# Two-choice mixture of experts on one core: result rows written straight to their tokens' places, and read in plain transfers at the end

## The chip, the cores and the metric

The kernel runs on one core of a Trainium2 chip. Its engines are TensorE (PE), VectorE (DVE), ScalarE (ACT), GpSimd (POOL) and SyncE (SP); 16 DMA engines serve it. SP and POOL issue the transfers. The metric is the device time of one execution in microseconds (us). A measurement of this kernel is the median of its runs.

## What is computed

A token block of 512 x 1024 floats runs through two blocks. The first is a conformer-like block (convolution, latent attention, convolutional feed-forward). The second has attention over selected keys, a gated delta rule, and a mixture of experts in two levels. The change lies in that last part. Cut to it, the reference is:

```python
top_gp, g_idx = lax.top_k(p_grp, 1)                       # one of 4 groups
top_pe, e_local = lax.top_k(softmax(in_grp), 2)           # 2 of its 8 experts
gates = top_pe / sum(top_pe) * top_gp
e_idx = g_idx * 8 + e_local                               # [512, 2]
...
hb = silu(xb @ w_gate[e]) * (xb @ w_up[e])                # each expert, on its tokens
yb = (hb @ w_down[e]) * gate
out = zeros(...).at[token].add(yb)                        # both choices of a token
...
x = layer_norm(alpha * x + (1 + gt2) * out, ln_g, ln_b)
```

Each of the 32 experts has three matrices of 2 MB (gate and up 1024 x 512, down 512 x 1024), 201 MB together, and each is used once.

## The kernel before

**Places.** Routing (`routing`, to L1740) gives every expert CAP = 64 places. Choice j of token p in token block t (4 blocks of 128) gets the row number `rows_i[p, j, t]`, cast at L1730: expert times 64 plus its rank among that expert's tokens. An expert with more than 64 tokens goes on in a loop behind (`overflow`, L1819, a `For_i` at L1823 with a run-time count, which starts with a barrier of all engines); there are 15 spare blocks for it.

**Expert loop** (from L1846). One pass per expert. `gate_up` (L1774) multiplies the tokens of the expert with the gate and up weights, 32 matmuls at L1782 (`gu`), and applies the activation (ACT L1787, DVE L1788). `down` (L1792) of the expert before is woven in: transposes (L1796), matmuls at L1805 (`py`), then the product with a modulation row into half of a 128 x 1024 tile `ey` (DVE L1811), which holds both experts of a pair. Weights come through `ld` and `ew` (L1556 to L1580): 12 tiles of 512 KB per expert, 384 in all, issued by SP (L1563 gate and up, L1565 down) into `eraw` buffers in the order of their use, each when its buffer is free and at most eight in flight. `ahead(e, n)` issues the first n of them early; before the overflow loop, at expert 16, it issues 15 tiles.

**Results.** `y_d` in DRAM has one row for each of the (32 + 15) x 64 places. At step i == 7 of every even expert from 2 on, POOL writes the `ey` tile of the pair before with one plain transfer of 512 KB (L1896), empty places too: 15 writes. The last pair (experts 30 and 31) stays on chip: it is split into two parts (`yh`, `yl`) and brought to its tokens by one-hot matmuls. Rows from 15 x 128 on, which this pair and the spare blocks would have, were filled with zeros much earlier by two transfers on SP (L918).

**Tail** (from L1915). Behind the last write, POOL issues eight gathers (L1920): for token block t and choice j, 128 rows of `y_d` picked by `rows_i` into a tile `ya`. `add(t, j)` (DVE L1925) adds gate times `ya` to the residual `x`. For t = 0 and 1 the second choice goes over PE instead, as a multiplication with a diagonal matrix of the gates (`dg`, L1941, into the accumulator `fin`). `sums(t)` adds the last pair's rows (L1946) and `x` (L1948) there. Then moments (DVE L1955), the norm (L1964 on), and `finish(t)` (ACT L1977, DVE L1978 and L1979, output by SP at L1980).

What sets the order: each engine works its own list in program order; SP's list holds the weight tiles and at its end the outputs, POOL's the writes and gathers.

Of the kernel before, what the change touches and what calls it, by code (L numbers as in the profile page):

```python
# [20 lines left out]
S = 512  # L21
# [28 lines left out]
def tile_model(ctx: ExitStack, tc: tile.TileContext, A: dict, out: bass.AP):  # L50
# [38 lines left out]
    def r(ap):  # L89
        return ap.bitcast(F32R)  # L90
# [820 lines left out]
            yield c  # L911


    y_d = dram.tile([(32 + 15) * 64, D], F32, name="y_d")
    zt = ch("zt")
    GP.memset(zt, 0.0)
    for hf in range(2):
        SY.dma_start(y_d[15 * P :, hf * S : (hf + 1) * S].rearrange("(a p) n -> p a n", p=64),  # L918
                     zt[:64, :].rearrange("p (o n) -> p o n", o=1).to_broadcast([64, 17, S]))

# [379 lines left out]
                    topk_some(1)  # L1302
    topk_some(1000)

    ckv = []
    for j in range(2):
        ps = col_T(w2, 1024 + j * P, h, "ckv")
# [383 lines left out]
    def routing():  # L1691

        ge, gs, e2 = rt(4, "ge"), rt(1, "gs"), rt(1, "e2")
        tc.keep_in_program_order(V.tensor_tensor(ge, gl, bc(gm, 4), ALU.subtract))
        SC.activation(ge, ge, AF.Exp)
        tc.keep_in_program_order(V.tensor_tensor(e2, m2, m1, ALU.subtract))
        SC.activation(e2, e2, AF.Exp)
        tc.keep_in_program_order(V.tensor_reduce(gs, ge, axis=AX.X, op=ALU.add))
        V.reciprocal(gs, gs)
        tc.keep_in_program_order(V.tensor_scalar(gate1, e2, 1.0, None, ALU.add))  # L1700
        V.reciprocal(gate1, gate1)
        V.tensor_tensor(gate1, gate1, gs, ALU.mult)
        V.tensor_tensor(gate2, gate1, e2, ALU.mult)

        nbi = rs_(NE).bitcast(I32)
        nb = rs_(NE)
        V.tensor_scalar(nb, pc, -1.0, 0.0, ALU.add, ALU.max)
        V.tensor_copy(nbi, nb)
        V.tensor_scalar(nbi, nbi, 6, None, ALU.arith_shift_right)
        V.tensor_copy(nb, nbi)  # L1710
        oend = [nb, rs_(NE), rs_(NE)]
        cur = 0
        for i, sft in enumerate((1, 2, 4, 8, 16)):
            nxt = 1 + i % 2
            V.tensor_copy(oend[nxt][:, :sft], oend[cur][:, :sft])
            V.tensor_tensor(oend[nxt][:, sft:], oend[cur][:, sft:], oend[cur][:, : NE - sft], ALU.add)
            cur = nxt
        oe = oend[cur]

        obase = rs_(NE)  # L1720
        V.tensor_tensor(obase, oe, nb, ALU.subtract)
        V.tensor_scalar(obase, obase, float(CAP), float(NE * CAP - CAP), ALU.mult, ALU.add)
        V.tensor_tensor(obase, obase, sbase, ALU.subtract)
        V.tensor_scalar(rowt, rk, float(CAP), None, ALU.is_ge)
        V.tensor_tensor(rowt, rowt, b3(obase), ALU.mult)
        V.tensor_tensor(rowt, rowt, rankf, ALU.add)
        for j in range(2):
            V.tensor_tensor(rj[j], rowt, E[j], ALU.mult)
            V.tensor_reduce(rowf[:, j, :], rj[j], axis=AX.X, op=ALU.add)
        V.tensor_copy(rows_i, rowf)  # L1730

        ovf = small(16, "ovf")[0:1, :]
        ovc = rs_(NOV * NE)[0:1].rearrange("p (b e) -> p b e", b=NOV)
        V.tensor_tensor(ovc, oe[0:1, :].rearrange("p (o e) -> p o e", o=1).to_broadcast([1, NOV, NE]),
                        iota[0:1, :NOV].rearrange("p (b o) -> p b o", o=1).to_broadcast([1, NOV, NE]), ALU.is_le)
        V.tensor_reduce(ovf[:, 0:NOV], ovc, axis=AX.X, op=ALU.add)
        V.tensor_scalar(ovf[:, 0:NOV], ovf[:, 0:NOV], float(NE - 1), None, ALU.min)
        V.tensor_copy(ovf[:, 15:16], oe[0:1, NE - 1 : NE])
        V.tensor_copy(ovi, ovf)
        V.tensor_scalar(relv, rflat, -float(NE * CAP), None, ALU.add)  # L1740

    gate1, gate2 = rt(1, "gate1", keep=True), rt(1, "gate2", keep=True)
    rowf = cpool.tile([P, 2, NT], F32, name="rowf")
# [76 lines left out]
    def overflow():  # L1820

        n_ov = nc.values_load(ovi[0:1, 15:16], min_val=0, max_val=NOV)
        with tc.For_i(0, n_ov, 1) as ib:  # L1823
            ei = nc.values_load(ovi[0:1, bass.ds(ib, 1)], engines=(mybir.EngineType.SP,), min_val=0, max_val=NE - 1)
            dyn = lambda w, q: ew({"g": wg, "u": wu, "d": wd}[w][bass.ds(ei, 1)].rearrange("o k n -> (o k) n"), 1 if w == "d" else 2, q, loop=True)
            xo, go = [], []
            run(gather(relv, 1, xo))
            run(gate_up(dyn, (xo[0], 0), go))
            yo = ytile()
            run(down(dyn, go[0], yo[:CAP, :]))  # L1830
            SY.dma_start(y_d[bass.ds(ib * CAP + NE * CAP, CAP), :], yo[:CAP, :])
            V.tensor_scalar(relv, relv, -float(CAP), None, ALU.add)

    def residual():
# [15 lines left out]
    for e in range(NE):  # L1850
# [31 lines left out]
            next(gx[0])  # L1882
            next(gx[0])
        if e == E_OV:
            ahead(e, 15)
            overflow()
            gx.append(gather(rel_cols((e // 4 + 1) * 4 * CAP), 4, xg))
        load = lambda w, q, e=e: ld(w, e, q)
        gu = gate_up(load, (xg[e // 4], e % 4), g)
        for i in range(8):  # L1890
            next(gu)
            if i == 2 and e:
                downs.append(down(loadp, gp, yp, rg=rgs[:, 0:1] if e == NE - 1 else None))
            downs = [d for d in downs if next(d, 1) is None]
            if i == 7 and e and e % 2 == 0:
                GP.dma_start(y_d[(e - 2) * CAP : e * CAP, :], yd)  # L1896
            if e >= E_RES and i % 4 == 3:
                next(res_, None)
            n = e % 4 * 8 + i
            if e == 0:  # L1900
                if i < 3:
                    next(gx[0])
                    next(gx[0])
            elif e < NE - 4 and (n >= 20 if e < 4 else n % 3 == 0):
                next(gx[-1], None)
# [11 lines left out]
    for t in range(NT):  # L1917
        for j in range(2):
            ya = pp("pa" if j == 0 else "pb", "ya")
            GP.indirect_dma_start(out=ya, out_offset=None, in_=y_d, in_offset=bass.IndirectOffsetOnAxis(ap=rows_i[:, j, t : t + 1], axis=0))  # L1920
            yas.append(ya)

    def add(t, j):
# [12 lines left out]
            split_to(yh[q, hs], yl[q, hs], y[q, hs])  # L1936
    pf = {(t, half): mm("fin") if t < 2 else acc("fin") for t in range(NT) for half in range(2)}
    HS = [slice(half * S, (half + 1) * S) for half in range(2)]
    for t in range(2):
        for half in range(2):  # L1940
            kp(PE.matmul(pf[t, half], lhsT=dg[:, cs[t]], rhs=yas[2 * t + 1][:, HS[half]], start=True, stop=False))  # L1941

    def sums(t):
        for half in range(2):
            for i, yy in enumerate((yh, yl)):
                kp(PE.matmul(pf[t, half], lhsT=r(ohT)[:, cs[t]], rhs=r(yy)[:, HS[half]], start=t > 1 and i == 0, stop=False))  # L1946
        for half in range(2):
            kp(PE.matmul(pf[t, half], lhsT=ident, rhs=x_sb[t][:, HS[half]], start=False, stop=True))  # L1948

# [29 lines left out]
            V.tensor_tensor(f, f, lb2[:, hs], ALU.add)  # L1979
            SY.dma_start(out[0, t * P : (t + 1) * P, hs], f)  # L1980

    for j in range(2):
        add(2, j)
    sums(0)
    moments(0)
    for j in range(2):
        add(3, j)
    sums(1)
    moments(1)
    norm((0, 1))  # L1990
    for t in (2, 3):
        sums(t)
        moments(t)
    finish(0)
    norm((2, 3))
    for t in (1, 2, 3):
# [15 lines left out]
```

## Time and profile before

| | us |
|---|---|
| runs | 2093.14, 2095.64, 2089.97 (median 2093.14) |
| profiled execution | 2092.43 |
| its span in the trace | 2090.7 |
| PE busy | 1988.3 (95%) |
| VectorE busy | 1241.0 (59%) |
| ScalarE busy | 756.4 (36%) |
| POOL busy | 78.4 (4%) |

The span is the time from the first to the last record of the profiled execution; the execution's own time is 1.7 us longer. "Busy" is an average over stages with different limits. The share of DMA in a window is the mean busy share of the 16 DMA engines; full engines show a share slightly over 1. "<-" behind an idle time names what ended it.

### The profile page before, as it was taken

Reading aid. Unit: us, or ns where it says so; the run is one execution under the profiler, and the core shown is the slowest. Engines: PE = TensorE matmul, PEld = TensorE weight load, DVE = VectorE, ACT = ScalarE, POOL = GpSimd, SP = SyncE. Lnnn points to the kernel's source line nnn. Section 1 sums busy time; section 2 is a strip of 40 time slices with the busy share of each in tenths; the row PEclk is TensorE's granted clock in tenths of the full one; section 3 lists DMA queues with packets and bytes.
Section 4 is the critical chain, followed back from the end, with each engine's and each line's share of the span. In section 5 each row is a group of like instructions: output and inputs, shape, how many; then the busy total and the mean of one; then the engine's idle time right before and its main releaser. Section 6 shows DMA issues by size and latency. Waiting matters only on the chain. (4 is left out here: it accounts for less than half of the span.)

```text
span 2090.7 us, 25944 instructions
## 1 busy us (share of the span) xinstructions
PE 1988.3 (95%) x9522; PEld 1397.1 (67%) x9522; DVE 1241.0 (59%) x2824; ACT 756.4 (36%) x1401; POOL 78.4 (4%) x110
## 2 busy tenths in 40 slices
PE   7999989999999999999999999999979999799985
PEld 6887658877877778888878877778754334333322
DVE  4898666688558747889999553443562221242216
ACT  5433873343223336755546234552230000000001
POOL 1000000000000011000000000010100000000001
PEclk9999999999999999999999999999989999899998
DMA  4443005366446335632232323133179999999994
GB/s 132 107 106 82 30 21 164 109 199 185 150 133 183 124 104 136 167 80 56 75 80 71 85 78 84 51 102 99 54 264 419 406 419 419 369 419 419 419 420 193
DMA packets 306342, 377.05 MB, mean 180 GB/s; under 512 B 45829, under 2 KB 225549, under 8 KB 306213
## 3 DMA queue, kind: packets, MB, share of 16 engines
q1 hardware_dynamic: 301748, 359.12, 50.6%
q0 software_dynamic: 4464, 16.25, 2.0%
q8 instruction: 76, 1.25, 0.2%
q14 instruction: 54, 0.43, 0.1%
HBM read 354.06 MB, written 21.26 MB: 180 GB/s over the span
## 5 line engine op out<-in xcount | busy, mean ns | idle before, releaser
L100 DVE TENSOR_TENSOR wl<-wraw,wh 128x1024 fp32r<-128x1024 f32 (+1 forms) x196 | 236.9, 1210 | 210.4 <-ACT wh L99 209.6
L99 ACT CAST wh<-wraw 128x1024 fp32r<-128x1024 f32 (+1 forms) x196 | 202.7, 1037 | 396.6 <-PE up L130 72.8
L1782 PE MATMUL gu<-eraw,xs 128*64 128x512 f32 x1024 | 316.1, 605 | 17.4 <-SPq L1823 11.8
L1782 PEld LDWEIGHTS gu<-eraw,xs 128*64 128x64 f32 x1024 | 83.0, 137 | 146.4 <-issue 109.2
L129 PE MATMUL pc<-hi,wh 128*128 128x512 f32 (+2 forms) x480 | 176.9, 374 | 0.8 <-ACT hi L99 0.4
L130 PE MATMUL pc<-lo,wh 128*128 128x512 f32 (+2 forms) x480 | 173.3, 364 | 0.5 <-DVE lo L100 0.5
L131 PE MATMUL pc<-hi,wl 128*128 128x512 f32 (+2 forms) x480 | 172.8, 362 | 0.0
L1805 PE MATMUL py<-eraw,ehT 128*64 128x512 f32 x512 | 162.5, 600 | 6.2 <-DMA eraw<-in_w_down_dram 4.6
L1788 DVE TENSOR_TENSOR eg<-gu,eg 64x512 f32<-64x512 f32 x32 | 22.2, 693 | 208.8 <-ACT eg L1787 208.5
L129 PE MATMUL up<-hi,wh 128*128 128x512 f32 x328 | 130.9, 399 | 0.0
L130 PE MATMUL up<-lo,wh 128*128 128x512 f32 x328 | 129.7, 395 | 0.0
L131 PE MATMUL up<-hi,wl 128*128 128x512 f32 x328 | 129.7, 395 | 0.0
L1787 ACT ACTIVATE eg<-gu 64x512 f32<-64x512 f32 x32 | 18.9, 589 | 279.0 <-PE gu L1782 279.0
L131 PEld LDWEIGHTS pc<-hi,wl 128*128 128x128 f32 (+1 forms) x480 | 90.1, 188 | 12.6
L129 PEld LDWEIGHTS pc<-hi,wh 128*128 128x128 f32 (+1 forms) x480 | 90.0, 189 | 12.6 <-ACT hi L99 1.0
L130 PEld LDWEIGHTS pc<-lo,wh 128*128 128x128 f32 (+1 forms) x480 | 90.4, 189 | 11.3 <-DVE lo L100 0.7
L1805 PEld LDWEIGHTS py<-eraw,ehT 128*64 128x64 f32 x512 | 45.1, 137 | 76.3 <-issue 56.7
L450 DVE SCALAR_TENSOR_TENSOR u<-u,cols_dw 128x497 f32<-128x497 f32 (+14 forms) x120 | 84.9, 753 | 0.7
L1770 ACT ACTIVATE xs<-xg,pb,pg 128x256 f32<-128x256 f32 x32 | 18.1, 564 | 177.8 <-PE xg L1766 161.7
L1766 PEld LDWEIGHTS xg<-oh,zNh 128*128 128x128 f32 x224 | 42.5, 190 | 53.1 <-issue 38.9
L129 PEld LDWEIGHTS up<-hi,wh 128*128 128x128 f32 x328 | 61.6, 188 | 23.8 <-ACT wh L99 7.8
L1772 DVE TENSOR_SCALAR xs<-xg,pg,pb 128x256 f32<-128x256 f32 x32 | 17.4, 543 | 95.4 <-PE xg L1766 95.3
(616 smaller groups left out, 4375.9 us busy)
## 6 DMA issues: line engine op xcount, KB each, us to landing
eraw<-in_w_gate_dram SPq DMA_DIRECT2D x128, 512.0 KB
eraw<-in_w_up_dram SPq DMA_DIRECT2D x128, 512.0 KB
eraw<-in_w_down_dram SPq DMA_DIRECT2D x128, 512.0 KB
wraw<-in_w_in_dram SPq DMA_DIRECT2D x91, 512.0 KB
wada<-in_w_ada_dram SPq DMA_DIRECT2D x48, 512.0 KB
wraw<-in_w_ffn_up_dram SPq DMA_DIRECT2D x44, 512.0 KB
wraw<-in_w_ffn_down_dram SPq DMA_DIRECT2D x20, 512.0 KB
wraw<-in_w_out_dram SPq DMA_DIRECT2D x16, 512.0 KB
```

The source lines that it names most:

```text
L99: c = SC.copy(r(hi), src)
L100: (eng or V).tensor_tensor(r(lo), src, hi, ALU.subtract)
L129: PE.matmul(ps, lhsT=wh, rhs=xh, start=start, stop=False)
L130: PE.matmul(ps, lhsT=wh, rhs=xl, start=False, stop=False)
L131: PE.matmul(ps, lhsT=wl, rhs=xh, start=False, stop=stop)
L450: yield lambda j=j, lo=lo, hi=hi, s=s: V.scalar_tensor_tensor(a[:, lo:hi], u[:, lo + s : hi + s], dww[:, j * 4 + c : j * 4 + c + 1], a[:, ...
L1766: PE.matmul(ps[:, :n], lhsT=hN[t][s_][:, c * P : (c + 1) * P], rhs=r(ov[:, t, :]), start=t == 0 and s_ == 0, stop=t == NT - 1 and s_ == 1)
L1770: SC.activation(xs[:, c], pv, AF.Identity, scale=pg[:, c : c + 1], bias=pb[:, c : c + 1])
L1782: PE.matmul(ps[m * CAP : (m + 1) * CAP, :], lhsT=xs[0][:, 2 * q + k, xs[1], :], rhs=rw[m][:, k * S : (k + 1) * S], start=q == 0 and k == 0 ...
L1787: SC.activation(g[CAP:, :], ps[:CAP, :], AF.Silu)
L1788: V.tensor_tensor(g[:CAP, :], ps[CAP:, :], g[CAP:, :], ALU.mult)
L1805: PE.matmul(py[half * CAP : (half + 1) * CAP, :], lhsT=hT[:, c * CAP : (c + 1) * CAP], rhs=raw[:, half * S : (half + 1) * S], start=c == 0 ...
```

## The change

`y_d` becomes 1024 rows, one for each choice of each token: row 2 x token + j. A table `tab_d` in DRAM with one integer per place says which row a place belongs to. It is filled with 2048, beyond the last row (1023), near the start of the second block. In `routing`, eight indirect writes put the row numbers of 128 tokens each into the table, and one read brings the first 2048 entries on chip as `tab` (128 x 16, a column per pair). The write of a pair (`put`, L1762 of the changed kernel) is an indirect write by such a column with a bounds check: a place whose entry is out of range is skipped. The zero fill covers all of `y_d`, moves behind the delta rule's stage and goes by POOL's queue. The tail reads `y_d` with eight plain transfers on SP, issued behind the last weight tile. On PE the second choice of all four token blocks goes over the diagonal matrix, and VectorE adds only the first choice. Before the overflow loop 13 tiles are issued ahead instead of 15. In that loop the write goes by the table too.

```diff
-    y_d = dram.tile([(32 + 15) * 64, D], F32, name="y_d")
+    y_d = dram.tile([2 * S, D], F32, name="y_d")
+
+    NROWS = (32 + 15) * 64
+    tab_d = dram.tile([NROWS, 1], I32, name="tab_d")
     zt = ch("zt")
     GP.memset(zt, 0.0)
-    for hf in range(2):
-        SY.dma_start(y_d[15 * P :, hf * S : (hf + 1) * S].rearrange("(a p) n -> p a n", p=64),
-                     zt[:64, :].rearrange("p (o n) -> p o n", o=1).to_broadcast([64, 17, S]))
+    ft = ch("ft").bitcast(I32)
+    GP.memset(ft, 4 * S)
+    GP.dma_start(tab_d.rearrange("(p a) o -> p (a o)", p=64), ft[:64, : NROWS // 64])
...
+    z2 = ch("z2")
+    GP.memset(z2, 0.0)
+    for hf in range(2):
+        GP.dma_start(y_d[:, hf * S : (hf + 1) * S].rearrange("(a p) n -> p a n", p=P),
+                     z2.rearrange("p (o n) -> p o n", o=1).to_broadcast([P, 2 * S // P, S]))
...
         V.tensor_copy(rows_i, rowf)
 
+        val = rs_(2 * NT).bitcast(I32).rearrange("p (j t) -> p j t", j=2)
+        GP.iota(val, pattern=[[1, 2], [2 * P, NT]], base=0, channel_multiplier=2)
+        for t in range(NT):
+            for j in range(2):
+                GP.indirect_dma_start(out=tab_d, out_offset=bass.IndirectOffsetOnAxis(ap=rows_i[:, j, t : t + 1], axis=0),
+                                      in_=val[:, j, t : t + 1], in_offset=None)
+        GP.dma_start(tab[:, : NE // 2], tab_d[: NE * CAP, :].rearrange("(k p) o -> p (k o)", p=P))
...
+    def put(y, idx):
+
+        GP.indirect_dma_start(out=y_d, out_offset=bass.IndirectOffsetOnAxis(ap=idx, axis=0), in_=y, in_offset=None,
+                              bounds_check=2 * S - 1, oob_is_err=False)
...
-            ahead(e, 15)
+            ahead(e, 13)
...
             if i == 7 and e and e % 2 == 0:
-                GP.dma_start(y_d[(e - 2) * CAP : e * CAP, :], yd)
+                put(yd, tab[:, e // 2 - 1 : e // 2])
...
             ya = pp("pa" if j == 0 else "pb", "ya")
-            GP.indirect_dma_start(out=ya, out_offset=None, in_=y_d, in_offset=bass.IndirectOffsetOnAxis(ap=rows_i[:, j, t : t + 1], axis=0))
+            SY.dma_start(ya, y_d.rearrange("(t p j) n -> t j p n", t=NT, j=2)[t, j])
...
-    for t in range(2):
+
+    def second(t):
         for half in range(2):
             kp(PE.matmul(pf[t, half], lhsT=dg[:, cs[t]], rhs=yas[2 * t + 1][:, HS[half]], start=True, stop=False))
 
+    second(0)
+    second(1)
+
     def sums(t):
+        if t > 1:
+            second(t)
...
-    for j in range(2):
-        add(2, j)
-    sums(0)
-    moments(0)
-    for j in range(2):
-        add(3, j)
-    sums(1)
-    moments(1)
-    norm((0, 1))
-    for t in (2, 3):
+    add(2, 0)
+    add(3, 0)
+    for t in range(NT):
         sums(t)
         moments(t)
+        if t == 1:
+            norm((0, 1))
```

Names ending in a number below are buffers. On POOL, between the routing and the first writes (`padr` is a routing buffer, `gt` the modulation row), the program was:

```order
L1541 MEMSET padr 128x120 [waits DMAHW4_49,DMAHW5_49,DMAHW3_49,DMAHW6_49,DMAHW2_49,DMAHW7_49,PE_49,Activation_49]
L1752 TENSOR_SCALAR gt_13229<-gt_13229 128x512 [waits DMAHW6_49,DMAHW5_49]
L1896 DMA y_d<-ey_13233 128x1024 [waits DVE_49]
L1896 DMA y_d<-ey_13441 128x1024 [waits DVE_49]
L1896 DMA y_d<-ey_13661 128x1024 [waits DVE_49]
```

and is now (of the eight L1744 rows the first two and the last stand here):

```order
L1549 MEMSET padr 128x120 [waits DMAHW2_49,DMAHW3_49,DMAHW1_49,DMAHW4_49,DMAHW0_49,DMAHW5_49,PE_49,Activation_49]
L1741 IOTA scr_13212 128x8
L1775 TENSOR_SCALAR gt_13236<-gt_13236 128x512 [waits DMAHW4_49,DMAHW3_49]
L1744 DMA tab_d<-scr_13212,rows_i 3008x1 [waits DMASW0_49,DVE_49,Pool_49]
L1744 DMA tab_d<-scr_13212,rows_i 3008x1 [waits DMASW3_49]
L1744 DMA tab_d<-scr_13212,rows_i 3008x1 [waits DMASW2_49,DMASW1_49]
L1746 DMA tab<-tab_d 128x16x1 [waits DMASW2_49]
L1762 DMA y_d<-ey_13240,tab 1024x1024 [waits DMASW3_49,DVE_49]
L1762 DMA y_d<-ey_13458,tab 1024x1024 [waits DMASW4_49,DVE_49]
```

The nine issues of the table stand ahead of the first pair's write, which waits for the read of the table (DMASW3).

At the end of the results' way, POOL's list was (last write, then the gathers):

```order
L1896 DMA y_d<-ey_15956 128x1024 [waits DVE_49]
L1920 DMA ya_16269<-y_d,rows_i 128x1024 [waits DMASW4_49,DMASW3_49,DMASW5_49,DMASW2_49,DMASW6_49,DMASW1_49,DMASW7_49,DMASW0_49,PE_49]
L1920 DMA ya_16271<-y_d,rows_i 128x1024 [waits PE_49]
L1920 DMA ya_16273<-y_d,rows_i 128x1024 [waits PE_49]
L1920 DMA ya_16275<-y_d,rows_i 128x1024 [waits PE_49]
L1920 DMA ya_16277<-y_d,rows_i 128x1024 [waits PE_49]
L1920 DMA ya_16279<-y_d,rows_i 128x1024 [waits PE_49]
L1920 DMA ya_16281<-y_d,rows_i 128x1024 [waits PE_49]
L1920 DMA ya_16283<-y_d,rows_i 128x1024 [waits PE_49]
```

and SP's list now ends so (`eraw` the last weight tiles, `ya` the reads; the sixth row is the last read):

```order
L1573 DMA eraw_16316<-in_w_down_dram 128x1024 [waits DMAHW4_49,PE_49]
L1573 DMA eraw_16318<-in_w_down_dram 128x1024 [waits DMAHW5_49,PE_49]
L1945 DMA ya_16320<-y_d 128x1024 [waits DMAHW6_49,DMASW3_49]
L1945 DMA ya_16322<-y_d 128x1024 [waits DMAHW7_49]
L1945 DMA ya_16324<-y_d 128x1024 [waits DMAHW0_49]
L1945 DMA ya_16334<-y_d 128x1024 [waits DMAHW5_49]
L2011 DMA out_dram<-x_12641 128x512 [waits DMAHW6_49,DVE_49]
```

The reads moved from behind the writes on POOL to behind the last weights on SP; the first waits for the last write (DMASW3), each for a free place among eight transfers.

On VectorE, in the tail, before (`ey`, `yhl` the last pair's rows, `x` the residual, `bn` moments):

```order
L1925 SCALAR_TENSOR_TENSOR x_12635<-ya_16269,r_gate_13223,x_12635 128x1024 [waits DMASW7_49]
L1925 SCALAR_TENSOR_TENSOR x_12638<-ya_16273,r_gate_13223,x_12638 128x1024 [waits DMASW1_49]
L100 TENSOR_TENSOR yhl_16306<-ey_16133,yhl_16305 64x512 [waits Activation_49] x2
L1925 SCALAR_TENSOR_TENSOR x_12641<-ya_16277,r_gate_13223,x_12641 128x1024 [waits DMASW3_49]
L1925 SCALAR_TENSOR_TENSOR x_12641<-ya_16279,r_gate_13224,x_12641 128x1024 [waits DMASW4_49,DVE_49]
L1955 BN_STATS bn_16335<-fin_16315 128x6 [waits PE_49]
L1955 BN_STATS bn_16335<-fin_16316 128x6 [waits PE_49]
L1925 SCALAR_TENSOR_TENSOR x_12644<-ya_16281,r_gate_13223,x_12644 128x1024 [waits DMASW5_49]
L1925 SCALAR_TENSOR_TENSOR x_12644<-ya_16283,r_gate_13224,x_12644 128x1024 [waits DMASW6_49,DVE_49]
L1955 BN_STATS bn_16346<-fin_16317 128x6 [waits PE_49]
```

and now:

```order
L100 TENSOR_TENSOR yhl_16357<-ey_16182,yhl_16356 64x512 [waits Activation_49] x2
L1836 SCALAR_TENSOR_TENSOR ey_16182<-py_16345,rg_16053,gt_13236 64x512 [waits PE_49]
L1950 SCALAR_TENSOR_TENSOR x_12641<-ya_16320,r_gate_13230,x_12641 128x1024 [waits DMAHW6_49]
L1836 SCALAR_TENSOR_TENSOR ey_16182<-py_16345,rg_16053,gt_13236 64x512
L1950 SCALAR_TENSOR_TENSOR x_12644<-ya_16324,r_gate_13230,x_12644 128x1024 [waits DMAHW0_49]
L1950 SCALAR_TENSOR_TENSOR x_12647<-ya_16328,r_gate_13230,x_12647 128x1024 [waits DMAHW2_49]
L1950 SCALAR_TENSOR_TENSOR x_12650<-ya_16332,r_gate_13230,x_12650 128x1024 [waits DMAHW4_49]
L1986 BN_STATS bn_16386<-fin_16366 128x6 [waits PE_49]
L1986 BN_STATS bn_16386<-fin_16367 128x6 [waits PE_49]
L1986 BN_STATS bn_16395<-fin_16368 128x6 [waits PE_49]
```

The two additions of the second choice (`r_gate_13224`) are gone, and the first two additions stand among and behind the last pair's rows.

## Rows read from the trace of the kernel before

**Rows 1.** The page: GB/s in the 40 slices of the span (52.3 us each).
```profile
GB/s 132 107 106 82 30 21 164 109 199 185 150 133 183 124 104 136 167 80 56 75 80 71 85 78 84 51 102 99 54 264 419 406 419 419 369 419 419 419 420 193
```

**Rows 2.** Windows: stretch, us, busy us of each engine (instructions), PE clock, DMA share, GB/s.
```profile
1850.00:1950.00 100.00, 99.46 (x447) 39.34 (x448) 22.29 (x43) 7.49 (x13) 1.59 (x3) 1.00 1.03 419
2000.00:2020.00 20.00, 16.21 (x56) 4.16 (x56) 2.49 (x4) 0.59 (x1) 0.00 (x0) 1.00 1.03 419
```

**Rows 3.** Timeline of ScalarE, experts four apart: start, duration, line, operands.
```profile
1893.40 0.59 ACT L1787 ACTIVATE eg<-gu 64x512 f32<-64x512 f32 x1 [8.98 <-PE gu L1782]
...
1953.69 0.59 ACT L1787 ACTIVATE eg<-gu 64x512 f32<-64x512 f32 x1 [8.98 <-PE gu L1782]
```

**Rows 4.** The chain of waits, 1985 us to the tail: start, duration, engine and line.
```profile
1985.53 0.65 PE rg L1870 x19
1986.18 9.91 DMA eraw<-in_w_up_dram
...
2055.19 1.98 PE py L1805 x4
2057.16 5.22 PE fin L1941 x8
```

**Rows 5.** The tail: two windows, and VectorE's timeline.
```profile
2057.20:2068.30 11.10, 11.10 (x28) 5.84 (x29) 9.26 (x11) 1.23 (x2) 0.00 (x0) 0.86 0.05 22
2068.30:2087.70 19.40, 4.66 (x14) 2.18 (x12) 17.69 (x54) 5.57 (x8) 0.00 (x0) 0.73 0.22 81
...
2065.68 2.59 DVE L1925 SCALAR_TENSOR_TENSOR x<-ya,r_gate,x 128x1024 f32<-128x1024 f32 x2
...
2086.34 1.29 DVE L1979 TENSOR_TENSOR x<-x,xs 128x512 f32<-128x512 f32 x2
```

**Rows 6.** Window right behind the last weight.
```profile
2055.19:2060.00 4.81, 4.81 (x8) 1.65 (x9) 2.68 (x4) 1.23 (x2) 0.00 (x0) 0.50 0.51 206
```

**Rows 7.** Instructions on y_d: duration ns min/median/max, first and last start; DMA landing times.
```profile
L1896 POOL DMA_DIRECT2D y_d<-ey x15: 531/531/620, 1591.4 to 2031.1; - x15
L1920 POOL DMA_INDIRECT ya<-y_d,rows_i x8: 937/940/1034, 2038.8 to 2047.6; - x8
...
DMA to landing us min/median/max: 6.7/7.1/12.4
```

**Rows 8.** Timelines of VectorE (row numbers), then POOL (last write, first and last gather).
```profile
1558.34 0.15 DVE L1730 CAST rows_i<-rowf 128x8 int32<-128x8 f32 x1
...
2031.09 0.53 POOL L1896 DMA_DIRECT2D y_d<-ey  x1 [32.53 <-DVE ey L1811]
2038.75 1.03 POOL L1920 DMA_INDIRECT ya<-y_d,rows_i  x1 [7.13 <-DMA y_d<-ey]
...
2047.59 0.94 POOL L1920 DMA_INDIRECT ya<-y_d,rows_i  x1 [0.30 <-issue]
```

**Rows 9.** Small elements: two windows, and their DMA issues (count, size).
```profile
908.00:911.00 3.00, 3.00 (x15) 2.41 (x14) 2.96 (x9) 1.29 (x2) 0.00 (x0) 1.00 0.42 56
1382.00:1387.00 5.00, 5.00 (x26) 3.51 (x25) 1.94 (x8) 3.28 (x7) 1.73 (x2) 1.00 0.81 173
...
simg<-DX SPq DMA_DIRECT2D x4, 64.0 KB
...
pv<-mod_d SPq DMA_DIRECT2D x2, 4.0 KB
...
pv<-in_ln_g_dram SPq DMA_DIRECT2D x1, 4.0 KB
pv<-in_ln_b_dram SPq DMA_DIRECT2D x1, 4.0 KB
```

**Rows 10.** PE in front of the overflow loop (L1823).
```profile
1802.41 1.98 PE L1782 MATMUL gu<-eraw,xs 128*64 128x512 f32 x4 [11.78 <-SPq L1823]
```

**Rows 11.** Zero fill: SyncE's next issue (start, duration), and the window.
```profile
827.28 21.55 SPq L1011 DMA_DIRECT2D simg<-zt  x4
...
830.00:850.00 20.00, 18.99 (x84) 14.35 (x84) 14.34 (x26) 10.40 (x20) 0.43 (x2) 1.00 0.98 195
```

More of the change, by code (lines that the diff above doesn't have):

```diff
@@ L1740, in routing @@
         V.tensor_scalar(relv, rflat, -float(NE * CAP), None, ALU.add)
+    tab = ep2.tile([P, P], I32, name="tab")
+    def put(y, idx):
+        GP.indirect_dma_start(out=y_d, out_offset=bass.IndirectOffsetOnAxis(ap=idx, axis=0), in_=y, in_offset=None,
+                              bounds_check=2 * S - 1, oob_is_err=False)
     gate1, gate2 = rt(1, "gate1", keep=True), rt(1, "gate2", keep=True)
@@ L1830, in overflow @@
             run(down(dyn, go[0], yo[:CAP, :]))
-            SY.dma_start(y_d[bass.ds(ib * CAP + NE * CAP, CAP), :], yo[:CAP, :])
+            idx = small(1, "idx", dt=I32)[:CAP, :]
+            SY.dma_start(idx, tab_d[bass.ds(ib * CAP + NE * CAP, CAP), :])
+            put(yo[:CAP, :], idx)
             V.tensor_scalar(relv, relv, -float(CAP), None, ALU.add)
@@ L1938, in tile_model @@
     HS = [slice(half * S, (half + 1) * S) for half in range(2)]
-    for t in range(2):
+    def second(t):
         for half in range(2):
             kp(PE.matmul(pf[t, half], lhsT=dg[:, cs[t]], rhs=yas[2 * t + 1][:, HS[half]], start=True, stop=False))
+    second(0)
+    second(1)
     def sums(t):
+        if t > 1:
+            second(t)
         for half in range(2):
             for i, yy in enumerate((yh, yl)):
-                kp(PE.matmul(pf[t, half], lhsT=r(ohT)[:, cs[t]], rhs=r(yy)[:, HS[half]], start=t > 1 and i == 0, stop=False))
+                kp(PE.matmul(pf[t, half], lhsT=r(ohT)[:, cs[t]], rhs=r(yy)[:, HS[half]], start=False, stop=False))
         for half in range(2):
```

## The prediction

> **What bounds the kernel now.** I read the slices of the page first, for the stage that the change sits in. From about 1570 us on the slices show close to 419 GB/s [rows 1]: the stage that streams the experts' weights, and everything the change touches except the fills lies in it or behind it. The windows come second: in 1850 to 1950 us and in 2000 to 2020 us all 16 DMA engines are full (share 1.03) at 419 GB/s [rows 2]. PE looks full too in the first of them (99.46 of 100 us) but not in the second (16.21 of 20). So the two are nearly balanced, and I compared their needs for four experts. PE: the same activation (L1787) of experts four apart starts at 1893.40 and 1953.69 us, 60.29 us [rows 3]. DMA: four experts are 48 tiles of 0.524 MB, at 419 GB/s 60.07 us, and two result writes of the same size each add 2 x 1.25, which make 62.57. DMA is slower by 2.3 us in every four experts, and PE lives on the tiles loaded ahead until these are used up. The chain of waits says when: 1985.53 us is its last piece of PE work before it goes over to weights, and it stays on them till 2055.19 us [rows 4]. From there PE needs 1.98 us for the last matmuls. Call 2055.19 T, the time of the last weight. After T comes a tail of 2090.70 - 2055.19 = 35.5 us that no load sets: VectorE is busy 9.26 of 11.10 and 17.69 of 19.40 us in it and ends at 2086.34 + 1.29 = 2087.63 us [rows 5]; 3 us of output follow.
>
> So the time is: DMA work from 1570 us to T, plus the tail. DMA work is not quite over at T: the next 4.81 us still move 206 GB/s [rows 6], 0.99 MB or 2.36 us at the full rate. All DMA work of the stage ends in effect at 2057.55 us.
>
> **Result writes (L1896 becomes an indirect write, L1762).** Before, 15 writes carry 512 KB each [rows 7], 15 x 1.25 = 18.8 us of all engines. I took the routing of the reference on its inputs: the 30 experts concerned hold 954 of 1920 places, no expert over 60, so 966 rows are skipped and the overflow loop stays empty. What skipping saves is in no row. The most is their bytes' time, 966/1920 x 18.8 = 9.4 us, if all 16 engines lose alike. The least is 0: filled places are the first 12 to 60 of each half of 64, so if one engine carries mainly low places it keeps its work, and the others wait for it; or a skipped row costs as much as a written one. I take the middle, 4.7 us, since neither even nor fully uneven fits such a filling, and keep both ends.
> The page "DMA: Bandwidth & Descriptors" of the Trainium skill (The descriptor swizzle) gives four neighbouring partitions to one engine in turn, a pair of such groups per half; by that rule the fullest engine keeps 89 of its 120 rows on these counts, an estimate of 4.85 us saved, against 9.4 if all engines gained alike. No row here shows the mapping.
> Issuing: the indirect reads take POOL 0.94 us each against 0.53 for plain writes [rows 7]. 15 x 0.41 = 6.2 us on POOL, which sits idle 32.53 us before such a write [rows 8]: hidden. The result buffer that the write must free is needed again one pair (30 us) later, far beyond the landing time of 6.7 to 12.4 us.
>
> **Table (new).** Eight scatters of 128 four-byte elements and one read of 2048 such elements, 3072 small packets, all before the first result write (1591.4 us, and the table is needed only there). Nearest rows: four loads of 4 KB in 8-byte pieces, 2048 packets, in a window of 5 us at 173 GB/s and share 0.81 [rows 9]. At the share-to-rate ratio of rows 2 the bytes explain 0.42 of the share, so the packets took 0.39 x 5 = 1.9 us. And 2048 written packets of 64 bytes took 0.42 x 3 = 1.3 us [rows 9]. So 2048/2048 x 1.9 for the read, and 1024/2048 x 1.3 = 0.6 for the scatters: 2.5 us; a part falls before 1570 us, where engines are still partly free. I take 2. Bounds: 0 and, if a small packet costs what a 4 KB one does (15 x 128 rows in 18.8 us, so 3072 would take 30), 30 us. The same page of the Trainium skill (its table of properties) says that transfers below 512 bytes become read-modify-writes, which speaks against this step; it gives no price, and no run here shows one.
> On POOL nine more issues of about 1 us precede the first write; from the row numbers (1558.49 us) to that write 33 us are there [rows 7, 8]: hidden.
>
> **Result reads (L1920 gathers on POOL become plain reads on SP, L1945).** Eight of 512 KB, 4.19 MB, 10.0 us at the full rate. Before, they were issued from 2038.75 to 2047.59 us [rows 8] and so went in between the last weights. Now they stand behind all weights on SP, so T comes earlier by as much as they had taken ahead of it, and they move behind T:
> T = 2057.55 - 4.7 (skipped rows) + 2.0 (table) - 10.0 (reads) = 2044.85 us, 10.3 earlier.
> The first read waits also for the last result write. That was issued at 2031.09 us and its reader waited till 2038.75 [rows 8], 7.7 us. It follows the weights, which by then are 2.4 us ahead (14 of the 15 savings, less the table), so it goes out at about 2028.7; even the slowest landing of 12.4 us [rows 7] ends at 2041.1. T is 3.8 us later, and the reads would not start before T anyway. So this wait is covered by 3.8 us; a landing later than that costs one to one.
>
> **Tail.** Reads now land from T + 1.25 to T + 10. VectorE makes four additions behind T as before: those of the second choice of t = 2 and 3 go to PE, and the first two, which before were made ahead of T, come behind it. The last addition waits for the seventh read, T + 8.75, and ends at T + 10.1; in the old tail the last one ended at 2068.27, T + 13.1 [rows 5]. PE in return gets the multiplications with the gate's diagonal of two more blocks of tokens. The two blocks of now take 5.22 us [rows 4], at a low clock; at the clock after that some 3 us, and its sums end near T + 20.7 instead of T + 17.8, under VectorE's norm and first finish. I get a VectorE end of T + 32.0 against T + 32.4, and a tail of 35.1 us. If PE's clock, granted at 0.50 right behind T [rows 6], stays low, the sums come later: up to + 5.
>
> **Rest.** The barrier in front of the overflow loop: 13 tiles go ahead instead of 15, so 2 tiles (2.5 us) go behind it. DMA work is the same and SP pauses as long as before; PE, which waited 11.78 us [rows 10], starts about 3 us earlier. That adds to its slack, (20 - 16.21)/20 x 70 us = 13 us between 1985 and 2055 [rows 2]: about 16 us, over the 10.3 by which T moves. Zero fill: 4.46 MB stood on SP from 825.8 us and held the next issue for 21.55 us, yet PE was busy 18.99 of 20 us there [rows 11]: taking it out gives 0 to 1 us. The new fill (4.2 MB, on POOL's queue in the attention stage) has weights beside it at some 80 GB/s [rows 1], so there is room: 0.
>
> **Sum.** Span T + 35.1 = 2080.0 us, and the run lies 2092.43 - 2090.70 = 1.7 above its span: 2081.7, rounded to 2081.5, 11 us below the profiled run. The median of the runs, 2093.14, is 0.7 above that run, so nothing is corrected.
>
> **Rivals.**
> *B: skipped rows free all engines alike.* Saving 9.4 instead of 4.7: 2077. T would move 15, still under PE's 16. For it: the rows are real bytes. Against: the filling is uneven by place.
> *C: skipping saves nothing*, because the write does not do what it says, or because the fullest engine keeps its rows: 2086.4. For it: nothing in the trace shows a skipped packet. Against: rows that are not moved should leave some engine time.
> *D, slower: the table's packets.* Place: the full engines at 1565 to 1590 us. 3072 packets are 192 per engine. The rows price one at 10 to 15 ns; the gain of 13 us without the table is gone at 13/192 = 68 ns, and the kernel is slower by 0.3% from 100 ns. At the upper bound of 30 us for the table: 2110. For it: four-byte elements occur nowhere in this trace as writes to scattered places. Against: both neighbouring rows are ten times cheaper than a 4 KB packet's 157 ns.
>
> **Numbers.** A measurement of this kernel can tell about 0.3%, 6.3 us, from no change: below 2086.9 is faster, above 2099.4 slower. Forecast 0.55; B 0.2; C 0.19, most of it within 0.3%, since it lies half a microsecond from the bound and the table or the clock can take that; D 0.06, nearly all of it slower. So faster 0.75, same 0.2, slower 0.05. The range runs from 2075 (B, with the microsecond of the old fill) to 2089 (C, with 2 to 3 us of a low clock).
>
> **What would show it.** The last weight should land near 2045 us, the eight reads behind it without a gap; the chain should stay on weights up to there. The result writes should show about half their packets, and the last window before T 419 GB/s of weights alone. A gap in DMA share between 1560 and 1590 us over 2.5 us would speak for D; T near 2049.5 for C, near 2040 for B. I am wrong in kind if the first read waits for the last write beyond T, if PE is late at T, or if the tail grows by over 5 us.

## The result, and the profile after

| | before | changed |
|---|---|---|
| median of 5 runs, us | 2090.7 (2088.77 to 2095.64) | 2080.7 (2079.67 to 2082.86) |
| ratio, 95% interval | | 0.9949 (0.9937 to 0.9960) |
| profiled execution, its span, us | 2092.43, 2090.7 | 2079.95, 2078.2 |

The kernel is faster by 0.51% (10.0 us); 2081.5 us was forecast, 11.6 below the 2093.14 known then (two more runs put the old kernel's median at 2090.7). The sum came out, but the profile shows that it did so with terms of another size.

Windows of the changed kernel that answer to [rows 2, 5]: DMA is as full as before, and behind the matmuls of the experts VectorE is again busy nearly all the time (13.23 of 13.84 and 13.76 of 15.02 us).

```profile
1850.00:1950.00 100.00, 98.99 (x443) 39.25 (x440) 23.70 (x43) 8.08 (x14) 2.92 (x3) 1.00 1.03 419
2000.00:2020.00 20.00, 16.52 (x60) 4.88 (x58) 2.49 (x4) 0.59 (x1) 0.00 (x0) 1.00 1.03 419
2046.16:2060.00 13.84, 13.84 (x38) 6.91 (x39) 13.23 (x30) 1.73 (x3) 0.00 (x0) 1.00 0.26 107
2060.00:2075.02 15.02, 3.99 (x12) 1.79 (x10) 13.76 (x36) 5.09 (x8) 0.00 (x0) 0.77 0.28 105
```

SyncE's timeline: the five last weight tiles, then the eight reads. The last read is issued at about 2041.7 us (the end of its group less one issue); it takes the place of the last weight among the eight transfers, so that weight has landed then. T was 2055.19 [rows 4], so it moved by 13.5 us; 10.3 were forecast.

```profile
2025.91 6.25 SPq L1573 DMA_DIRECT2D eraw<-in_w_down_dram  x5
2033.04 9.01 SPq L1945 DMA_DIRECT2D ya<-y_d  x8
```

But the chain of waits no longer ends on that weight:

```profile
2024.70 10.78 DMA eraw<-in_w_up_dram
2035.53 1.50 PE gu L1805 x5
2037.03 0.37 PE py L1828
2037.50 0.60 ACT eg L1810
2038.12 0.70 DVE eg L1811
2038.85 0.74 DVE ey L1836
2039.62 0.76 DVE ey L1836
2040.41 0.44 DVE ehT L1821
2040.89 5.25 PE py L1828 x16
2046.16 0.74 DVE ey L1836
```

It hangs on the last *up* weight, which arrives at 2035.53. Behind it come the last gate and up matmuls, the activation, two VectorE products of the expert before, the copy of the transposed tile, and 16 down matmuls without a wait, up to 2046.14: 10.6 us. The loads of the five down tiles behind that up tile need only 5 x 1.25 = 6.25 us. In the chain of the kernel before, the last weight was under way for 16.56 us from its issue, with the gathers beside it, and the matmuls waited for it:

```profile
2038.59 16.56 DMA eraw<-in_w_down_dram
```

Now it takes some 9.9 us (issued at 2031.8, landed near 2041.7).

PE in front of the overflow loop waits 4.00 instead of 11.78 us [rows 10]:

```profile
1795.15 1.97 PE L1805 MATMUL gu<-eraw,xs 128*64 128x512 f32 x4 [4.00 <-SPq L1846]
```

POOL's timeline, table and writes:

```profile
1559.31 1.20 POOL L1744 DMA_INDIRECT tab_d<-scr,rows_i  x1 [20.17 <-issue]
1561.95 0.98 POOL L1744 DMA_INDIRECT tab_d<-scr,rows_i  x1 [1.44 <-DMA tab_d<-scr,rows_i]
...
1596.61 0.97 POOL L1744 DMA_INDIRECT tab_d<-scr,rows_i  x1 [4.80 <-DMA tab_d<-scr,rows_i]
1602.64 1.22 POOL L1746 DMA_DIRECT2D tab<-tab_d  x1 [5.07 <-DMA tab_d<-scr,rows_i]
1611.04 1.00 POOL L1762 DMA_INDIRECT y_d<-ey,tab  x1 [7.18 <-DVE eg L1811]
1628.83 0.98 POOL L1762 DMA_INDIRECT y_d<-ey,tab  x1 [16.78 <-DVE ey L1834]
...
2024.68 0.97 POOL L1762 DMA_INDIRECT y_d<-ey,tab  x1 [32.46 <-DVE ey L1834]
```

The eight scatters are a chain: each waits for the landing of the one before, from the third on for 3.9 to 5.4 us. The first result write goes out at 1611.04, 20 us later than before [rows 7]; the second, at 1628.83, is on time (1628.41 before). What the table moved, by the DMA view of 1559 to 1612 us (POOL's queue: packets, MB, share of 16 engines), and the first result write, by that of 1615 to 1619 us:

```profile
q0 software_dynamic: 304, 0.01, 0.7%
q0 software_dynamic: 144, 0.11, 8.4%
```

0.7% of 53 us is 0.4 us of all engines. That is not all of the table's price. Some 5 us behind the issue of its read, the weights come more slowly while the engines stay full; the same window in the changed kernel and in a run without the table (e12 below):

```profile
1607.00:1609.00 2.00, 2.00 (x12) 0.71 (x9) 0.45 (x1) 0.00 (x0) 0.00 (x0) 1.00 1.10 246
1607.00:1609.00 2.00, 2.00 (x12) 0.58 (x9) 0.52 (x2) 0.00 (x0) 0.00 (x0) 1.00 1.03 412
```

In the packet records, 52 weight packets of 4 KB take over 220 ns there instead of 159, which adds 0.9 us of all engines. Each of the twelve kernels with the table's read shows this (45 to 54 packets, 0.7 to 1.1 us); the old kernel and e12 have 2 such packets at that place. So the table takes 1.1 to 1.5 us; why its read slows other packets, no run shows.

The first write (27 filled places) moved 0.11 MB, 27 rows of 4 KB; in the packet records each of its 101 skipped rows is one packet of 4 bytes and 9 ns, against 159 ns for a row.

### The profile page after: what moved, and what is told of

Read it like the earlier page. It is cut to its first block, busy times and chain, and to the rows that moved or that the text cites. A ratio compares the mean times of both kernels' runs of the same rounds, so it can differ in the third digit from the quotient of the medians.

```text
span 2078.2 us, 26018 instructions
## 1 busy us (share of the span) xinstructions
PE 1990.9 (96%) x9530; PEld 1397.1 (67%) x9530; DVE 1239.0 (60%) x2822; ACT 756.9 (36%) x1401; POOL 90.3 (4%) x117
## 3 DMA queue, kind: packets, MB, share of 16 engines
q8 instruction: 76, 1.25, 0.2%
## 5 line engine op out<-in xcount | busy, mean ns | idle before, releaser
L1805 PE MATMUL gu<-eraw,xs 128*64 128x512 f32 x1024 | 318.3, 605 | 10.0 <-SPq L1846 4.0
L1805 PEld LDWEIGHTS gu<-eraw,xs 128*64 128x64 f32 x1024 | 83.1, 137 | 141.0 <-issue 99.7
```

What stands on the lines that cost most here:

```text
L1805: PE.matmul(ps[m * CAP : (m + 1) * CAP, :], lhsT=xs[0][:, 2 * q + k, xs[1], :], rhs=rw[m][:, k * S : (k + 1) * S], start=q == 0 and k == 0 ...
```

## The experiments

Each ratio below is to the old kernel measured beside the run (medians 2090.67 to 2091.47 us). Profiled executions reach the expert stage up to 7 us apart (its first matmul starts between 1547.8 and 1554.7 us), so I measure that stage by itself: from the start of the first gate or up matmul to the start of the last, the two times in the row of L1805 (L1782 before; another line number where an edit adds lines). It ends with the last up weight, ahead of the reads. It is one profile per kernel; kernels that should have the same stage differ by up to 1.6 us below.

### What skipping rows is worth

```diff
-    y_d = dram.tile([2 * S, D], F32, name="y_d")
+    y_d = dram.tile([2 * S + (32 + 15) * 64, D], F32, name="y_d")
...
-    GP.memset(ft, 4 * S)
+    GP.iota(ft[:64, : NROWS // 64], pattern=[[1, NROWS // 64]], base=2 * S, channel_multiplier=NROWS // 64)
...
-                              bounds_check=2 * S - 1, oob_is_err=False)
+                              bounds_check=2 * S + NROWS - 1, oob_is_err=False)
```

> Every place's row is written: empty places go to spare rows behind the 1024 real ones (the table is filled with spare row numbers instead of 2048), so each of the 15 writes moves 512 KB again. All else is the changed kernel. Theory A (a skipped row frees its time on all 16 DMA engines alike): the writes 3 to 15 fall where DMA is the clock and skip 799 of 1664 rows, 7.8 us; the lead of the weights over the old kernel at the end (6.45 us, by SyncE's last issues) shrinks to about 0, the last read is issued near 2048.5 us instead of 2041.7, and the time is 6 to 8 us above the changed kernel. Theory B (an engine's share of the rows is fixed by the place, and the fullest engine decides): 4.2 us instead of 7.8, last read near 2046, time 4 us above. Theory C (skipping saves nothing; the lead came from somewhere else): no change, last read at 2041.7.

Measured: 2087.41 us, 6.7 above the changed kernel (0.998 of the old kernel, 0.997 to 0.999). The stage, here, in the changed kernel and in the old one:

```profile
L1805 PE MATMUL gu<-eraw,xs x1024: 592/592/1117, 1547.8 to 2040.8; 128*64 128x512 f32 x171
```

```profile
L1805 PE MATMUL gu<-eraw,xs x1024: 592/592/1114, 1551.7 to 2036.9; 128*64 128x512 f32 x171
L1782 PE MATMUL gu<-eraw,xs x1024: 592/592/1116, 1551.7 to 2043.6; 128*64 128x512 f32 x171
```

493.0 us against 485.2, and 491.9 before. Three other runs below whose writes follow the same routed table (e4, e8, e11) have 484.4, 484.8 and 486.0:

```profile
L1805 PE MATMUL gu<-eraw,xs x1024: 592/592/1116, 1552.0 to 2036.4; 128*64 128x512 f32 x171
L1805 PE MATMUL gu<-eraw,xs x1024: 592/592/1112, 1554.5 to 2039.3; 128*64 128x512 f32 x171
L1805 PE MATMUL gu<-eraw,xs x1024: 592/592/1117, 1554.7 to 2040.7; 128*64 128x512 f32 x171
```

So skipping saves 7.0 to 8.6 us of the stage. C falls. B's 4.2 is too small, and A's 7.8 fits, which the next runs put in doubt again.

The four fixed patterns differ in one number, which is 4 here, and 32, 16 or 1 in the others (`y_d` has 2048 rows in them, and the bounds check goes to the last):

```diff
-        GP.dma_start(tab[:, : NE // 2], tab_d[: NE * CAP, :].rearrange("(k p) o -> p (k o)", p=P))
+        GP.dma_start(tab[:, 16:32], tab_d[: NE * CAP, :].rearrange("(k p) o -> p (k o)", p=P))
+        GP.iota(tab[:, 32:48], pattern=[[P, 16]], base=0, channel_multiplier=1)
+        V.tensor_scalar(tab[:, 48:64], tab[:, 32:48], 4, None, ALU.bitwise_and)
+        V.scalar_tensor_tensor(tab[:, :16], tab[:, 48:64], 4096.0, tab[:, 32:48], ALU.mult, ALU.add)
```

> The writes no longer follow the routing: a fixed pattern writes exactly the 64 of 128 places of every pair whose place number p has (p and 4) = 0, to rows of its own, and skips the other 64; the scatters and the table's read stay but are not used, and the tail adds rows that don't belong to its tokens. Both this run and the next write 960 rows in the 15 writes. Theory A (a skipped row frees all engines alike): the same time as the next run, and as the changed kernel within 1 us. Theory B (four neighbouring places go to one engine, in turn): places of this pattern lie on every second engine alone, so the fullest engines keep all 120 rows and nothing is saved: 7.5 us later in the last read's issue than the next run, and 6 to 8 us slower.

> As the run before, with the 64 places that have (p and 32) = 0. Theory A: the same as the run before. Theory B (four neighbouring places to one engine, in turn, eight engines for each half of 64): this pattern halves every engine's rows alike, so it saves the full half of the bytes: the last read issued a little before the changed kernel's 2041.7, near 2039 (7.5 against 4.2 us saved on writes 3 to 15), and 7.5 us before that of the run before.

> Fixed pattern again: of every pair's 128 places the 64 with (p and 16) = 0 are written, the others skipped; the tail adds rows that don't belong to its tokens. Theory B1 (four neighbouring places go to one engine, eight engines for each half of 64): p and 16 decides between two sets of engines, so half of the engines keep all their rows, nothing is saved, and the run is as slow as the one with (p and 4) = 0 (2087.0 us, lead of the weights at the end 2.1 us). Theory B2 (places go to the 16 engines in turn, one by one, p mod 16): every engine loses half its rows, and the run is as fast as the one with (p and 32) = 0 (2077.0 us, lead 9.8 us).

> As the run before, with the 64 places that have (p and 1) = 0. Theory B1: each group of four neighbours loses two, so every engine loses half: as fast as (p and 32) = 0, 2077 us, lead 9 to 10 us. Theory B2: the places of this pattern go to every second engine, which keep all their rows: as slow as (p and 4) = 0, 2087 us, lead about 2 us.

| written places | time, us | stage, us |
|---|---|---|
| all (e1) | 2087.41 | 493.0 |
| (p and 4) = 0 (e2) | 2087.03 | 492.4 |
| (p and 16) = 0 (e5) | 2088.36 | 492.4 |
| (p and 32) = 0 (e3) | 2077.04 | 482.4 |
| (p and 1) = 0 (e6) | 2079.24 | 483.6 |

The stages of e2, e5, e3 and e6:

```profile
L1808 PE MATMUL gu<-eraw,xs x1024: 592/592/1117, 1549.2 to 2041.6; 128*64 128x512 f32 x171
L1808 PE MATMUL gu<-eraw,xs x1024: 592/592/1113, 1552.8 to 2045.2; 128*64 128x512 f32 x171
L1808 PE MATMUL gu<-eraw,xs x1024: 592/592/1117, 1550.8 to 2033.2; 128*64 128x512 f32 x171
L1808 PE MATMUL gu<-eraw,xs x1024: 592/592/1117, 1552.4 to 2036.0; 128*64 128x512 f32 x171
```

Against e1, two patterns save 0.6 us of the stage and two 9.4 to 10.6, with the same 960 rows. Which rows are skipped decides, and not only how many. One result write under (p and 4) = 0 and under (p and 32) = 0, POOL's queue in the microsecond in which it moved most:

```profile
q0 software_dynamic: 47, 0.11, 27.0%
```

```profile
q0 software_dynamic: 40, 0.16, 39.8%
```

The first write takes little over a quarter of the 16 engines beside the weights, the second 40%. The packet records say why: in the writes of e2 and e5 at most 8 rows are under way at any moment, in those of e3 and e6 up to 15 and 14, and a row takes 159 ns in the median in all of them. A write of 64 rows lasts 2.5 us in the median under the slow patterns, as one of all 128 rows does in e1, and 1.4 and 1.8 us in e3 and e6. So under the slow patterns 8 engines carry all 64 rows. For a plain transfer of 1 MiB to 128 partitions, the page "DMA: Bandwidth & Descriptors" of the Trainium skill (The descriptor swizzle) gives four neighbouring partitions to one engine; the trace agrees for these indirect writes as to how many engines share each of the four patterns; which ones they are it does not show.

If the fullest engine sets the saving, giving out places in another order should save more:

```diff
+    GP.iota(ioi, pattern=[[32, 8], [1, 8], [8, 4]], base=0, channel_multiplier=0)
+    V.tensor_copy(iotap, ioi)
...
-                V.tensor_scalar(o1, iota[:, :n], rel[:, t : t + 1], None, ALU.is_equal)
+                V.tensor_scalar(o1, iotap[:, :n], rel[:, t : t + 1], None, ALU.is_equal)
...
+        V.tensor_scalar(pm, ri, 7, None, ALU.bitwise_and)
+        V.tensor_scalar(pq, ri, 3, 3, ALU.arith_shift_right, ALU.bitwise_and)
+        V.tensor_scalar(ri, ri, 5, 5, ALU.arith_shift_right, ALU.arith_shift_left)
+        V.scalar_tensor_tensor(ri, pm, 4.0, ri, ALU.mult, ALU.add)
+        V.tensor_tensor(ri, ri, pq, ALU.add)
```

> The 64 places of an expert are given out in another order: rank r takes place 32 (r / 32) + 4 (r mod 8) + (r / 8) mod 4, so that neighbouring ranks lie four places apart (a second list of column numbers for the one-hot gather, and five small operations on the row numbers before the scatters); the result is the same. Theory B (four neighbouring places to one engine, the fullest engine decides): the fullest engine then keeps 69 of its 120 rows instead of 89, which saves 51 x 0.156 = 8.0 us instead of 4.85; by that the time is 2 to 3 us below the changed kernel's 2080.7, and the lead of the weights at the end about 9 us instead of 6.5. Rival (the routed rows already free all engines nearly alike, since they saved 6.7 us in the time and not 4.85): at most 1 us faster.

(The table's tile also shrinks, from 128 to 16 columns.) Measured: 2081.14 us (0.9957, 0.9943 to 0.9970): no gain. The writes did become shorter (1.5 us in the median instead of 1.8), but the stage has 486.7 us, rather more than the changed kernel's 485.2:

```profile
L1817 PE MATMUL gu<-eraw,xs x1024: 592/592/1116, 1549.5 to 2036.2; 128*64 128x512 f32 x171
```

So rows go to engines in groups as stated, but "the fullest engine of the whole stage" is not how much the routed rows save: it gives 4.85 us where 7.0 to 8.6 were measured, and foretold 2 to 3 us more for the spread places, which brought none. What lets the routed rows save that much, and why even loads add nothing to it, stays open.

### The reads

```diff
-            SY.dma_start(ya, y_d.rearrange("(t p j) n -> t j p n", t=NT, j=2)[t, j])
+            GP.dma_start(ya, y_d.rearrange("(t p j) n -> t j p n", t=NT, j=2)[t, j])
```

> The eight plain reads go by POOL's queue right behind the last result write, as the gathers did, instead of behind the last weights on SyncE; all else is the changed kernel. Theory A (place matters, not the kind of read): the reads, released near 2032, move beside the last weights again; the last weight lands 6 to 9 us later (near 2049), the last matmuls of the experts end near 2051 instead of 2046.1, and the time is about 4 to 5 us above the changed kernel. Rival (what counted was that gathers became plain reads): no change beyond 1 us.

Measured: 2084.44 us (0.9966, 0.9955 to 0.9978), 3.7 above the changed kernel, with intervals that overlap by 0.0005; the profile tells more. PE waits for the last down weights again, the last of which lands at 2047.08 instead of about 2041.7:

```profile
2040.40 1.08 PE L1828 MATMUL py<-eraw,ehT 128*64 128x512 f32 x4 [1.56 <-DVE ehT L1821]
2041.64 1.08 PE L1828 MATMUL py<-eraw,ehT 128*64 128x512 f32 x4 [0.16 <-DMA eraw<-in_w_down_dram]
2044.16 1.08 PE L1828 MATMUL py<-eraw,ehT 128*64 128x512 f32 x4 [1.43 <-DMA eraw<-in_w_down_dram]
2047.08 1.98 PE L1828 MATMUL py<-eraw,ehT 128*64 128x512 f32 x4 [1.84 <-DMA eraw<-in_w_down_dram]
```

So the reads' place behind the weights brings this; what plain reads are worth against gathers in the same place, no run shows.

### The table

Against the run with (p and 32) = 0 (e3):

```diff
-        for t in range(NT):
-            for j in range(2):
-                GP.indirect_dma_start(out=tab_d, out_offset=bass.IndirectOffsetOnAxis(ap=rows_i[:, j, t : t + 1], axis=0),
-                                      in_=val[:, j, t : t + 1], in_offset=None)
-        GP.dma_start(tab[:, 16:32], tab_d[: NE * CAP, :].rearrange("(k p) o -> p (k o)", p=P))
```

> As the run with (p and 32) = 0, but without the eight scatters and the table's read: the fixed pattern needs none (the tail again adds rows that don't belong to its tokens). Theory (by the trace a scatter is 16 packets of 32 bytes at 15 ns and the read 32 packets of 256 bytes at 81 ns, under 0.5 us in all, and the late first write is hidden): the time stays within 1 us of 2077.0. Rival (the table costs the 2 us of the forecast): 2 us faster.

Measured: 2079.87 us (0.9948, 0.9933 to 0.9963), against 2077.04 with the table (0.9929, 0.9910 to 0.9948), on another chip; the stage has 482.7 against 482.4 us. Leaving the table out saves nothing that can be seen in the time; it is 2.8 us slower here, outside the 1 us expected and away from the rival. The 1.1 to 1.5 us read from the packets are too few for this comparison.

### The chain behind the last up weight, and the tail

```diff
-            if i == 2 and e:
+            if i == (7 if e == NE - 1 else 2) and e:
```

> Only the last expert's turn changes: its gate and up matmuls and weights come first, and the down part of the expert before it behind them (it was woven in). Theory: in the changed kernel the end hangs on the chain behind the last up weight (2035.53 us; activation, transposes, 16 matmuls till 2046.1) and no longer on the last weight (landed near 2041.7). With the last up weight some 4 tiles (5 us) earlier, the last expert's down matmuls follow the weights again and end about 2 us behind the last one, near 2043.7; the whole is 1.5 to 2.5 us faster than the changed kernel, about 2078.5 us. Rival (VectorE and the reads set the tail, whenever the matmuls end): no gain, within 0.7 us of 2080.7.

Measured: 2079.51 us (0.9942, 0.9928 to 0.9956), 1.2 below the changed kernel: short of the theory's 1.5 and beyond the rival's 0.7. The changed kernel's interval holds this, so no gain is shown. The chain did change: the last down matmuls are over by 2041.8 us, and what follows waits for a read:

```profile
2022.21 10.98 DMA eraw<-in_w_down_dram
2033.21 10.96 DMA ya<-y_d
2044.17 0.14 issue
2044.30 5.37 PE fin L1967 x8
```

PE's multiplications with the diagonal start at 2044.30 when the second read is there, against 2046.04 in the changed kernel. Of the rival, this much is shown: with the chain shortened, the reads behind the weights are next, 2.5 us behind the last matmuls.

Both edits, the spread places (e9) and this order (e7), in one kernel:

> The run before and the order of e7 (the last expert's gate and up part ahead of the down part before it) in one. If the two gains are of different places (DMA work up to the last weight; the chain behind the last up weight), they add: 1.2 us of e7 and 2 to 3 us, so 2076 to 2078. If the tail behind the reads takes the place, 2078 to 2079.5.

Measured: 2081.09 us (0.9954, 0.9941 to 0.9968), outside both ranges expected: the two edits together bring nothing either.

The second choice of two token blocks goes back to VectorE (e8):

```diff
     def sums(t):
-        if t > 1:
-            second(t)
...
-    add(2, 0)
-    add(3, 0)
     for t in range(NT):
+        if t < 2:
+            for j in range(2):
+                add(2 + t, j)
         sums(t)
```

> The second choice of token blocks 2 and 3 is added by VectorE again, as in the old kernel, and the multiplications with the diagonal are left to blocks 0 and 1; the plain reads and their place stay. Theory: VectorE paces the tail, so two additions of 1.28 us more on it, with the last one waiting for the last read, make the time 1.5 to 2.6 us longer than the changed kernel. Rival (PE's sums pace it, and four more multiplications of some 0.47 us a block half cost as much): no change, within 0.7 us.

Measured: 2082.7 us (0.9956, 0.9941 to 0.9972), 2.0 above the changed kernel. Behind the experts' last matmuls come 34.5 us (2048.7 to 2083.2) instead of 32.1. That the second choice of two blocks went to PE is worth about 2 us by both, though the two ratios' intervals overlap.

### The overflow barrier

```diff
-            ahead(e, 13)
+            ahead(e, 15)
```

> 15 tiles are issued ahead of the overflow loop, as before, instead of 13; all else is the changed kernel. Theory: PE's wait in front of the loop grows by the 2 tiles, from 4.0 to 6.5 us, DMA work is the same, and the end hangs on DMA: no change of the time, within 1 us. Rival (PE's time behind the barrier reaches the end): 2 to 2.5 us slower.

Measured: 2081.32 us (0.9949, 0.9933 to 0.9964): no change. PE waits 7.15 us instead of 4.00 (6.5 foretold), and it does not reach the end. The wait here, and in e1:

```profile
1801.45 1.98 PE L1805 MATMUL gu<-eraw,xs 128*64 128x512 f32 x4 [7.15 <-SPq L1846]
1795.63 1.98 PE L1805 MATMUL gu<-eraw,xs 128*64 128x512 f32 x4 [8.64 <-SPq L1846]
```

## Why the prediction was right, and which terms were not

The forecast had the last expert matmuls end at T + 1.98 = 2046.8 us and 33.1 us behind them; the profile has 2046.1 and 32.1. Its steps:

- **DMA sets the pace of the expert stage: right.** Writing all rows again costs 6.7 us and reading beside the weights 3.7, so both gains lie in the stage where the forecast looked for them, though not in its sizes. The zero fill was taken as 0: the stage starts at 1551.7 us in both profiles, but with starts up to 7 us apart this does not show it to a microsecond.
- **Skipped rows, 4.7 us: too small.** The runs show 7.0 to 8.6 us of the stage and 6.7 of the time, between the 4.7 and the 9.4 of rival B (even loss on all engines). The row that could have told was not there; the middle of two far bounds was a choice, and the truth lay above it.
- **Table, 2.0 us: too large, and partly for another reason.** Its own packets took 0.4 us of all engines, the weight packets that its read slowed 0.7 to 1.1 more. The price was taken from element-wise packets of 8 and 64 bytes, at 15 and 10 ns (the old kernel's packet records give 9 and 8), but a scatter of 128 elements shows 16 packets of 32 bytes and the read 32 of 256. "33 us are there, hidden" also failed, since the scatters wait for each other: from 1558 to the first write 52 us were needed. That cost nothing because the next write was due only at 1628.
- **Reads behind the weights, T earlier by what they had taken ahead of it: right in kind**, with 5.4 us of the last weight in e4 where 7.6 were forecast (the 10.0 less the 2.36 that still went behind T).
- **T sets the end: wrong.** With T 13.5 us earlier the end moved 11 us up to the last matmuls, since the chain behind the last up weight took over. The forecast looked at PE's slack over 70 us and found 16 us; the slack that counted was that of the last five tiles, 10.6 us of dependent work against 6.25 us of loads. This is one of the prediction's own signs of being wrong in kind, PE late at T: the last matmuls end 4.4 us behind T and not 1.98. T came 3.2 us earlier than forecast, and the chain took 2.5 us of it back. Two errors of opposite sign met, so that the sum came out within 1 us is luck.
- **Tail, 0.4 us shorter: 1.4 in the profiles**, and 2.0 by e8. The clock term (up to + 5) did not come in the tail: PE's granted clock is 1.00 in 2046 to 2060 us (the 2.4 GHz level), where it was 0.50 (1.2 GHz) right behind T before [rows 6].
- **Barrier: no effect on the time, right.** PE's wait fell by 7.8 us and not by 3: 3.2 from the two tiles (e11) and 4.6 from the skipped rows (e1 waits 8.64 us).

The clock fell ahead of the tail instead: behind a stretch in which PE was busy for 2.89 of 5 us, the mean granted clock is 0.69, between the two levels.

```profile
2036.00:2041.00 5.00, 2.89 (x16) 1.09 (x14) 2.75 (x5) 1.80 (x3) 0.00 (x0) 0.97 1.02 419
2041.00:2046.00 5.00, 5.00 (x16) 1.32 (x16) 1.15 (x2) 0.03 (x1) 0.00 (x0) 0.69 1.02 412
```

The 16 down matmuls take 5.22 us there; in e7, at 1.00, 20 take 4.87. So some 1.3 of the chain's 10.6 us are the clock's, an estimate from these rows (the changed kernel's, and e7's with its window):

```profile
2040.89 5.22 PE L1828 MATMUL py<-eraw,ehT 128*64 128x512 f32 x16 [1.56 <-DVE ehT L1821]
2034.43 4.87 PE L1828 MATMUL py<-eraw,ehT 128*64 128x512 f32 x20
2034.43:2039.30 4.87, 4.77 (x22) 1.19 (x20) 2.39 (x4) 1.08 (x2) 0.00 (x0) 1.00 1.01 412
```

## What to carry to other kernels

Where loads set the pace, put transfers that nothing needs yet behind them: reads that are due after the last weight cost least behind it. An indirect write that skips empty rows saves engine time, but ask which places are empty: skipping half the rows saved half the writes' time or nothing here, by their partition numbers alone. And when a bound moves by 10 us, price the short chain behind the last input that needs most work, and not the slack of the whole stage.

## What the runs showed of the hardware

- An indirect write of 128 rows keeps the engines by partition, written rows or not: with (p and 4) = 0 or (p and 16) = 0 no more than 8 rows are ever under way, with (p and 32) = 0 or (p and 1) = 0 up to 15; a row of 4 KB takes 0.159 us of its engine.
- A row out of bounds is still a packet, of 4 bytes and 9 ns.
- Skipping half the rows of 15 writes, those left being spread over all engines, shortened the stage by 9.4 to 10.6 us, a little more than the 9.4 us that their bytes take at the full rate.
- The page "DMA: Bandwidth & Descriptors" of the Trainium skill (its table of properties) has transfers below 512 bytes as read-modify-writes; the scatters' packets of 32 bytes took 15 ns each here, and no run shows a read-modify-write by itself.
- Reading 2048 single elements of 4 bytes from DRAM cost more than its own packets (32 of 256 bytes, 81 ns each): beside it 45 to 54 weight packets of 4 KB took over 220 ns instead of 159 in each of twelve kernels, 0.7 to 1.1 us of all engines.
